# Token tiles 2 to 9 loaded in a transposed layout as well, with 1/rms spread by one small product

## The chip, the core and the metric

The kernel runs on one core of one Trainium2 chip. The core has a matrix engine (TensorE, PE in the profile, with its weight loads as PEld), a vector engine (DVE), a scalar engine (ACT), GpSimd (POOL) and a queue that issues DMAs (SP). The metric is device time in microseconds, the median of several executions. All data are float32. Many products are split into three: a value is held as a high part that PE multiplies fast (fp32r) and a low part, the rest, and high x high, high x low and low x high are added up.

## The reference, cut to what matters

One layer of a backbone block: 1024 latent tokens (x) and 256 context tokens (ctx), 1024 channels. What the change touches is its first step, the norm and modulation ahead of the input projection:

```
def rms_norm(x, g):
    y = xf * lax.rsqrt(jnp.mean(xf * xf, axis=-1, keepdims=True) + EPS)
    return (y * g).astype(x.dtype)

def modulate(h, shift, scale):
    return h * (1.0 + scale) + shift

px = modulate(rms_norm(x, g_pre_mix), sh_m, sc_m) @ w_in
pc = modulate(rms_norm(ctx, g_pre_mix), csh_m, csc_m) @ w_in
...   (window attention and mLSTM on px and pc, output projection, SwiGLU)
```

scale and shift come from a conditioning vector through w_ada and are vectors over channels; 1/rms is one number for each token.

## The kernel before, in words

The opening stage reads w_ada, makes `scol` = g (1 + scale) and `hcol` = shift as columns over channels, and prepares the tokens in ten tiles of 128 (0 to 7 are x, 8 and 9 are ctx). The projections need the tokens transposed, channels on the partitions. For each tile i:

- `prep_a`: a DMA loads `xt` (128 tokens x 1024 channels). ACT squares it with a running sum (Square; the squares themselves go to `hraw` as waste) and takes the root, DVE the reciprocal: column 10+i of `st` is 1/rms of each token. POOL multiplies `xt` by it (for tile 2 ACT does it in `prep_a2`, for tile 3 POOL at L434).
- `prep_t`: PE transposes the eight 128x128 blocks of `xt` into two PSUM tiles `pt`.
- `prep_m`: DVE multiplies them by `scol` into `hraw` (L231, two halves of 128x512).
- `prep_b`: POOL adds `hcol` (L244, two halves; tiles 0 and 1 on DVE), ACT casts each half to the high part `hh` (`ch` for ctx), DVE subtracts for the low part `hl` (`cl`, L257). hh0, hl0 hold the first four channel blocks, hh1, hl1 the other four.

After that PE multiplies the tile with the first 272 columns of the projection (`s1`: 24 products into a PSUM tile `slab`, L77 to L79 in `mm3`, with `w1h`, `w1l`); DVE adds the gates' bias (`G`, L396 and L398), ACT copies the rest (`av`, `V`, L400 and L401). The next 384 columns (`s2`, `w2h`, `w2l`) fill in between, first half and second half of the channels apart. Their weights come by DMA in four pieces `wr384` and are split by ACT (L448) and DVE (L449).

Python issues tile i's product, prep_b of tile i+2 and prep_a of tile i+4 in one loop step (L423 on), but the order on each engine is set by a scheduler at build time, which works with its own estimates of durations; only instructions marked `keep_in_program_order` hold their place among each other. On the chip each engine runs its list in that order and waits at the head of it. SBUF buffers R4 to R15 are shared by tag: `xt` has R4 to R7, `hraw` R8 to R13 from tile 2 on, which held w_ada before, and the pieces of w2 R14 and R15. DMAs are issued by SP in order; one whose buffer is still read holds up those behind it. `tc.issue_after` puts a DMA behind another.

Of the kernel before, what the change touches and what calls it, by code (L numbers as in the profile page):

```python
# [9 lines left out]
F32 = mybir.dt.float32  # L10
F32R = mybir.dt.float32r
AF = mybir.ActivationFunctionType
ALU = mybir.AluOpType
PSUM = bass.MemoryType.PSUM
ADD, SUB, MUL, MAX, MIN = ALU.add, ALU.subtract, ALU.mult, ALU.max, ALU.min

P = 128
D = 1024
KT = D // P
S = 1024  # L20
NT = S // P
# [20 lines left out]
WSPLIT = {1: 3, 2: 6, 3: 7, 5: 0, 6: 4, 7: 1, 8: 2, 9: 5}  # L42


def body(tc, x, ctx, vecs, bcv, bada, gqm, gqf, wada, ws1, ws2, wt, wout, wfi, wfo,
         const, cosc, sinc, out):
    nc = tc.nc
    pe, act, dve, pool = nc.tensor, nc.scalar, nc.vector, nc.gpsimd
# [36 lines left out]
    def hcast(t, n=4, w=P):  # L85

        return t.rearrange("p (h o) -> p h o", o=1).broadcast_to([t.shape[0], n, w])
# [94 lines left out]
        act.activation(dst, ss, AF.Sqrt, bias=epst, scale=1.0 / D)  # L182
        dve.reciprocal(dst, dst)

    def prep_a2(i):
        tc.keep_in_program_order(act.activation(xts[i], xts[i], AF.Copy, scale=st[:, 10 + i:11 + i]))

    def prep_a(i, parts=(0, 1)):

        j = i - NT  # L190
        xt = xts[i] = R(4 + i % 4, f"xt{i}", (D,))
        xd[i] = dma(xt, x[i * P:(i + 1) * P] if i < NT else ctx[j * P:(j + 1) * P])
        hraw[i] = R((2, 3)[i] if i < 2 else (12, 13, 8, 9, 10, 11)[i % 6], f"hraw{i}", (KT, P))
        sq = act.activation(hraw[i].rearrange("p a b -> p (a b)"), xt, AF.Square, accum_out=st[:, i:i + 1])
        if i > 1:
            tc.keep_in_program_order(sq)
        if 1 not in parts:
            tc.keep_in_program_order(act.activation(st[:, 10 + i:11 + i], st[:, i:i + 1], AF.Sqrt, bias=epst, scale=1.0 / D))
            return
        rms_r(st[:, 10 + i:11 + i], st[:, i:i + 1])  # L200
        pool.tensor_scalar(xt, xt, st[:, 10 + i:11 + i], 1.0, MUL, MUL)

    pts = {}

    def prep_t(i, keep=False, parts=(0, 1)):

        xt = xts[i]
        for b in parts:
            pt = pa.tile([P, 4, P], F32, name="pt", tag="tp" if i else "mm", bufs=2 if i else 4)
            for k in range(4):  # L210
                kk = 4 * b + k
                t = pe.transpose(pt[:, k, :], xt[:, kk * P:(kk + 1) * P], ident)
                if keep and (not kk or i == 1):
                    tc.keep_in_program_order(t)
            pts.setdefault(i, []).append(pt)
# [3 lines left out]
    def prep_m(i):  # L219

        if i not in pts:
            prep_t(i)
        rw = hraw.pop(i)
        raw2[i] = [rw[:, 4 * b:4 * b + 4] for b in range(2)]
        for b in range(2):
            if i == 1 and not b:
                for k in range(4):
                    tc.keep_in_program_order(act.activation(raw2[i][b][:, k], pts[i][b][:, k], AF.Copy,
                                                                    scale=scol[:, 0, 4 * b + k:4 * b + k + 1]))
                continue  # L230
            r = dve.tensor_tensor(raw2[i][b], pts[i][b], hcast(scol[:, i // NT, 4 * b:4 * b + 4]), MUL)  # L231
            if i == 1:
                tc.keep_in_program_order(r)

    def prep_b(i):

        if i not in raw2:
            prep_m(i)
        q, j = (0, i) if i < NT else (1, i - NT)
        hs, ls = (hh, hl) if i < NT else (ch, cl)  # L240
        tok = slice(j * P, (j + 1) * P)
        raws_ = raw2.pop(i)
        for b in (1, 0) if i == 0 else range(2):
            r = (dve if i < 2 else pool).tensor_tensor(raws_[b], raws_[b], hcast(hcol[:, q, 4 * b:4 * b + 4]), ADD)  # L244
            if i < 2:
                tc.keep_in_program_order(r)
            if i == 0:
                w1_split(1, (1 - b,))
        for b in range(2):
            h_ = hs[b][:, :, tok]  # L250
            if i + b == 0:
                for k in range(4):
                    act.activation(h_[:, k], pts[i][b][:, k], AF.Identity, scale=scol[:, q, k:k + 1],
                                   bias=hcol[:, q, k:k + 1])
            else:
                tc.keep_in_program_order(act.copy(h_, raws_[b]))
            r = dve.tensor_tensor(ls[b][:, :, tok], raws_[b], h_.bitcast(F32), SUB)  # L257
            if i == 0:
                tc.keep_in_program_order(r)
        if i == 0:  # L260
            with tc.issue_after(last):
                prep_a(2, (0,))
            r2 = st[:, 12:13]
            tc.keep_in_program_order(dve.reciprocal(r2, r2))
            prep_a2(2)

    def slab_load(hi, lo, src, n, k0):
        for k in (0, 2):
# [154 lines left out]
    for i in range(NI):  # L423
        if i + 4 < NI:
            prep_a(i + 4)
        if i == 0:
            s1(i)
            prep_t(2, True)
        if i + 2 < NI:
            prep_b(i + 2)  # L430
        if i == 0:
            r = st[:, 13:14]
            dve.reciprocal(r, r)
            tc.keep_in_program_order(pool.tensor_scalar(xts[3], xts[3], r, 1.0, MUL, MUL))  # L434
        if i:
            s1(i)
        if i == 4:
            for m_, c_ in ((mF, up), (mB, lw)):
                tc.keep_in_program_order(dve.tensor_scalar(m_, c_, -1.0, -NEG, ADD, MUL))
        if i in (1, 2):  # L440
            b = i - 1
            w2h.append(w2_tile("h", b, f"w2h_{b}").rearrange("p (k n) -> p k n", k=4))
            w2l.append(w2_tile("l", b, f"w2l_{b}").rearrange("p (k n) -> p k n", k=4))
            with tc.issue_after(xd[i + 4].ins):
                for k in (0, 2):
                    raw = R(14 + k // 2, f"wr384_{k}", (2, 384))
                    dma(raw, ws2[:, b, k:k + 2])
                    tc.keep_in_program_order(act.copy(w2h[b][:, k:k + 2], raw))  # L448
                    dve.tensor_tensor(w2l[b][:, k:k + 2], raw, w2h[b][:, k:k + 2].bitcast(F32), SUB)  # L449
        if 3 <= i < 3 + 2 * NFILL:  # L450
            s2((i - 3) // 2, ((i - 3) % 2,))
# [1484 lines left out]
def pack(i):  # L1936
    a = {k: np.asarray(v) for k, v in i.items()}
    w = a["w_in"][0]
    aqw, akw, avw, mqw, mkw, mvw, mow, mgw = np.split(w, np.cumsum([512, 128, 128, 256, 256, 512, 512]), axis=1)
    cc = np.ascontiguousarray  # L1940

    def slab(z):
        return cc(z.reshape(2, 4, P, -1).transpose(2, 0, 1, 3))

    tiles = {}
    for j in range(4):
        tiles[f"aq{j}"] = np.concatenate([aqw[:, 64 * j:64 * j + 64], aqw[:, 256 + 64 * j:256 + 64 * j + 64]], 1)
        tiles[f"mo{j}"] = mow[:, 128 * j:128 * j + 128]
    for j in range(2):
        tiles[f"mq{j}"] = mqw[:, 128 * j:128 * j + 128]  # L1950
        tiles[f"mk{j}"] = mkw[:, 128 * j:128 * j + 128]
    tiles["ak"] = akw

    def ttile(z):
        return z.reshape(KT, P, P).transpose(1, 0, 2)

    conv = a["w_conv_qk"][0]
    vec = np.concatenate(
        [np.stack([a["c"][0].reshape(KT, P), a["c_ctx"].reshape(KT, P)], 0).transpose(2, 1, 0).reshape(P, 16),
         conv.reshape(3, 4, P).transpose(2, 1, 0).reshape(P, 12),  # L1960
         a["g_mlstm_out"][0].reshape(4, P).T]
        + [a["b_ada"][0].reshape(6, KT, P)[i].T for i in (0, 1, 3, 4)]
        + [a[k][0].reshape(KT, P).T for k in ("g_pre_mix", "g_pre_ffn")] + [np.eye(P, dtype=np.float32)], 1)
    wo = a["w_out"][0]
    wop = np.stack([np.concatenate([wo[64 * j:64 * j + 64], wo[256 + 64 * j:256 + 64 * j + 64]], 0) for j in range(4)]
                   + [wo[512 + 128 * j:640 + 128 * j] for j in range(4)], 0)
    fi = a["w_ffn_in"][0].reshape(KT, P, 2, HT, P).transpose(3, 2, 1, 0, 4)
    con, cos, sin = _consts()
    return {
        "x": cc(a["x"][0]), "ctx": cc(a["ctx"][0]), "vecs": cc(vec),  # L1970
        "bcv": np.concatenate([a["b_gates"][0], a["attn_sink"][0]])[None, :],
        "bada": cc(a["b_ada"]), "gqm": cc(a["g_post_mix"]), "gqf": cc(a["g_post_ffn"]),
        "wada": cc(a["w_ada"][0]),
        "ws1": slab(np.concatenate([mgw, avw, mvw[:, :128]], 1)), "ws2": slab(mvw[:, 128:]),
        "wt": cc(np.stack([ttile(tiles[n]) for n in TILES], 0)),
        "wout": cc(wop), "wfi": cc(fi), "wfo": cc(a["w_ffn_out"][0].reshape(HT, P, D)),
        "const": con, "cosc": cos, "sinc": sin,
    }
# [11 lines left out]
```

## Time and profile before

| | |
|---|---|
| three runs | 1181.67, 1182.40, 1182.69 us; median 1182.4 |
| profiled execution | 1181.93 us, span 1180.2 us, mean granted PE clock 0.998 |
| PE, PEld busy | 1161.6 us (98%), 948.0 us (80%) |
| DVE, ACT, POOL busy | 781.8 us (66%), 558.0 us (47%), 154.0 us (13%) |
| DMA | 214.89 MB, mean 182 GB/s |

The span is the time from the first to the last instruction of one execution under the profiler; all rows are from that execution. The token tiles are prepared between about 20 and 80 us of it. A row of the timeline gives start and length in us, engine, line, operation, output<-inputs, shapes, count, and in brackets how long the engine had been idle before it and what ended that. Lines are those of the kernel before.

### The profile page before, as it was taken

The numbers are of one execution on the slowest core, as the hardware profiler recorded it, in microseconds if no ns is written. First come the engines' busy times: TensorE is split into PE (matmuls) and PEld (weight loads), VectorE is DVE, ScalarE is ACT, GpSimd is POOL, SyncE is SP. The second block draws the span as 40 slices with busy tenths as digits, with TensorE's granted clock in tenths as the row PEclk, the third lists the DMA queues.
The fourth block names the chain that finished last, engine by engine and source line by source line (L and its number), as shares of the span: only waits on it lengthen the run. The fifth ranks groups of instructions, "written<-read, shape, count | busy, mean of one in ns | idle before, by whom it ended". The sixth has DMA issues, their size and how long they took to land.

```text
span 1180.2 us, 16216 instructions
## 1 busy us (share of the span) xinstructions
PE 1161.6 (98%) x5881; PEld 948.0 (80%) x5881; DVE 781.8 (66%) x1367; ACT 558.0 (47%) x1035; POOL 154.0 (13%) x204
## 2 busy tenths in 40 slices
PE   9899999999999999999999999999999999999997
PEld 3799888778787777888788888888888888888886
DVE  5863768872877752559767767777777755644566
ACT  6743442221776864887433333333333434434543
POOL 1550001225555550000000000000000000000000
PEclk9999999999999999999999999999999999999999
DMA  9611954747885733220344565655654558665853
GB/s 367 218 54 51 382 201 138 217 122 224 220 257 158 220 98 118 88 92 36 98 134 130 202 239 207 221 197 205 219 173 135 178 191 272 207 212 184 310 184 125
DMA packets 101992, 214.89 MB, mean 182 GB/s; under 512 B 10004, under 2 KB 39316, under 8 KB 100504
## 3 DMA queue, kind: packets, MB, share of 16 engines
q1 hardware_dynamic: 101912, 213.85, 54.9%
q8 instruction: 46, 0.75, 0.3%
q14 instruction: 34, 0.28, 0.1%
HBM read 157.19 MB, written 55.97 MB: 181 GB/s over the span
## 4 chain that ended last, share of the span: by engine, by line
PE 89%; DMA 4%; DVE 4%; ACT 1%; issue 1%; SPq 0%; POOL 0%; DVEq 0%; ACTq 0%
PE xv L79 8%; PE xv L77 8%; PE xv L78 8%; PE pt L77 6%; PE pt L78 6%; PE pt L79 6%; PE po L1019 3%; PE t L597 3%; PE t L596 3%; PE t L599 3%; PE pt L1001 3%; PE op L77 3%; PE op L79 2%; PE op L78 2%; PE fx L77 2%; PE slab L77 2%
## 5 line engine op out<-in xcount | busy, mean ns | idle before, releaser
L66 DVE TENSOR_TENSOR fo<-fr,fo 128x1024 fp32r<-128x1024 f32 x77 | 92.7, 1223 | 70.4 <-ACT fo L65 65.9
L65 ACT CAST fo<-fr 128x1024 fp32r<-128x1024 f32 x77 | 79.8, 1053 | 73.8 <-PE pt L79 33.1
L596 PE MATMUL t<-hh,th 128*128 128x512 f32 x208 | 82.4, 396 | 0.0
L597 PE MATMUL t<-hl,th 128*128 128x512 f32 x208 | 82.1, 395 | 0.0
L1396 ACT CAST wS<-wr 128x512 fp32r<-128x512 f32 x88 | 54.3, 624 | 55.2 <-PE pt L79 36.6
L1398 DVE TENSOR_TENSOR wS<-wr,wS 128x512 fp32r<-128x512 f32 x88 | 60.4, 689 | 19.8 <-ACT wS L1396 19.8
L77 PE MATMUL xv<-tT,wS 128*128 128x512 f32 x168 | 65.6, 391 | 0.0
L79 PE MATMUL xv<-tT,wS 128*128 128x512 f32 x168 | 65.6, 391 | 0.0
L78 PE MATMUL xv<-tT,wS 128*128 128x512 f32 x168 | 65.5, 390 | 0.0
L599 PE MATMUL t<-hh,tl 128*128 128x512 f32 x208 | 65.0, 393 | 0.0
L77 PE MATMUL op<-woh,mh 128*128 128x512 f32 x128 | 51.1, 399 | 0.0
L79 PE MATMUL op<-woh,ml 128*128 128x512 f32 x128 | 50.0, 391 | 0.0
L78 PE MATMUL op<-wol,mh 128*128 128x512 f32 x128 | 49.9, 390 | 0.0
L1144 DVE TENSOR_TENSOR wr<-wr 128x512 f32<-128x512 f32 x66 | 45.5, 689 | 1.4
L596 PEld LDWEIGHTS t<-hh,th 128*128 128x128 f32 x208 | 39.1, 188 | 8.3 <-issue 0.3
L597 PEld LDWEIGHTS t<-hl,th 128*128 128x128 f32 x208 | 39.1, 188 | 8.1 <-issue 1.4
L1430 ACT ACTIVATE es<-es 128x512 f32<-128x512 f32 x22 | 13.9, 634 | 66.5 <-DVE es L1147 66.5
L78 PE MATMUL pt<-fo 128*128 128x512 f32 x110 | 42.8, 389 | 0.0
L77 PE MATMUL pt<-fo 128*128 128x512 f32 x110 | 42.8, 389 | 0.0
L79 PE MATMUL pt<-fo 128*128 128x512 f32 x110 | 42.8, 389 | 0.0
L972 PE MATMUL s<-k,qh 128*128 128x256 f32 (+1 forms) x128 | 42.2, 339 | 0.6 <-DVE sm L974 0.5
L599 PEld LDWEIGHTS t<-hh,tl 128*128 128x128 f32 x208 | 37.3, 188 | 6.6 <-issue 0.3
(786 smaller groups left out, 3341.0 us busy)
## 6 DMA issues: line engine op xcount, KB each, us to landing
wr<-in_wfi SPq DMA_DIRECT2D x44, 512.0 KB, 4.5
wb<-in_wada SPq DMA_DIRECT2D x24, 512.0 KB, 5.6
s_d<-a SPq DMA_DIRECT2D x22, 512.0 KB, 6.8
bt<-in_wfo SPq DMA_DIRECT2D x44, 256.0 KB, 3.6
tb_d<-bt SPq DMA_DIRECT2D x11, 1024.0 KB, 3.9
fr<-s_d SPq DMA_DIRECT2D x44, 256.0 KB, 4.5
fr<-tb_d SPq DMA_DIRECT2D x44, 256.0 KB, 4.3
fr<-a_d SPq DMA_DIRECT2D x33, 256.0 KB, 3.7
```

Source lines behind the costliest of these rows:

```text
L65: act.copy(hi, raw)
L66: dve.tensor_tensor(lo, raw, hi.bitcast(F32), SUB)
L77: pe.matmul(ps, a[0], b[0], start=first, stop=False, **kw)
L78: pe.matmul(ps, a[0], b[1], start=False, stop=False, **kw)
L79: pe.matmul(ps, a[1], b[0], start=False, stop=last, **kw)
L596: pe.matmul(o, wh[:, kt], m[0], start=f, stop=False)
L597: pe.matmul(o, wh[:, kt], m[1], start=False, stop=False)
L599: pe.matmul(o, wl[:, kt], m[0], start=False, stop=l)
L972: pe.matmul(o, qh[:, h, :], k2[g][:, kc], start=True, stop=False)
L1144: dve.tensor_tensor(out, a, b, SUB)
L1396: act.copy(w[:, 0], raw)
L1398: dve.tensor_tensor(w[:, 1], raw, w[:, 0].bitcast(F32), SUB)
```

## The change

For tiles 2 to 9 a second copy of the tokens comes from memory in transposed layout (`xtr`, made when the inputs are packed: per tile 128 partitions x 8 channel blocks x 128 tokens, 512 KB) straight into `hraw`. `xt` is loaded as before, but only for the sum of squares, and Square writes its waste over `xt`. The eight transposes are replaced by one product: the column of 1/rms, spread over 128 columns, times the identity gives a PSUM tile in which every partition holds the 128 tokens' 1/rms. DVE multiplies all of `hraw` by it in one instruction (128x1024), and POOL does scale and shift at once, in eight instructions of 128x128, one for each channel block, with `scol` and `hcol` as its two column operands. The multiplications of `xt` by 1/rms go. Tiles 0 and 1 stay as they are.

```diff
-def body(tc, x, ctx, vecs, bcv, bada, gqm, gqf, wada, ws1, ws2, wt, wout, wfi, wfo,
+def body(tc, x, ctx, xtr, vecs, bcv, bada, gqm, gqf, wada, ws1, ws2, wt, wout, wfi, wfo,
...
-    def prep_a2(i):
-        tc.keep_in_program_order(act.activation(xts[i], xts[i], AF.Copy, scale=st[:, 10 + i:11 + i]))
     def prep_a(i, parts=(0, 1)):
...
-        sq = act.activation(hraw[i].rearrange("p a b -> p (a b)"), xt, AF.Square, accum_out=st[:, i:i + 1])
+        if i > 1:
+            xd[i] = dma(hraw[i], xtr[i])
+        sq = act.activation(xt if i > 1 else hraw[i].rearrange("p a b -> p (a b)"), xt, AF.Square, accum_out=st[:, i:i + 1])
...
-        pool.tensor_scalar(xt, xt, st[:, 10 + i:11 + i], 1.0, MUL, MUL)
+        if i < 2:
+            pool.tensor_scalar(xt, xt, st[:, 10 + i:11 + i], 1.0, MUL, MUL)
     def prep_t(i, keep=False, parts=(0, 1)):
         xt = xts[i]
+        if i > 1:
+            pts[i] = pa.tile([P, 4, P], F32, name="pt", tag="tp", bufs=2)[:, 0]
+            t = pe.matmul(pts[i], st[:, 10 + i:11 + i].broadcast_to([P, P]), ident, start=True, stop=True)
+            if keep:
+                tc.keep_in_program_order(t)
+            return
...
         raw2[i] = [rw[:, 4 * b:4 * b + 4] for b in range(2)]
+        if i > 1:
+            dve.tensor_tensor(rw, rw, pts[i].rearrange("p (o t) -> p o t", o=1).broadcast_to([P, KT, P]), MUL)
+            return
...
-            r = (dve if i < 2 else pool).tensor_tensor(raws_[b], raws_[b], hcast(hcol[:, q, 4 * b:4 * b + 4]), ADD)
-            if i < 2:
-                tc.keep_in_program_order(r)
+            if i > 1:
+                for k in range(4):
+                    kk = 4 * b + k
+                    pool.tensor_scalar(raws_[b][:, k], raws_[b][:, k], scol[:, q, kk:kk + 1], hcol[:, q, kk:kk + 1], MUL, ADD)
+                continue
+            tc.keep_in_program_order(dve.tensor_tensor(raws_[b], raws_[b], hcast(hcol[:, q, 4 * b:4 * b + 4]), ADD))
...
-            prep_a2(2)
...
-            tc.keep_in_program_order(pool.tensor_scalar(xts[3], xts[3], r, 1.0, MUL, MUL))
...
+        "xtr": cc(np.concatenate([a["x"][0], a["ctx"][0]], 0).reshape(NT + NC_, P, KT, P).transpose(0, 3, 2, 1)),
```

The scheduler's order changes on all engines in this stage; behind it every engine's list is the same as before. Names carry the number of the tile or piece, and slab_442, slab_564 and slab_628 are the first products of tiles 1, 3 and 4 after the change.

DVE around the low parts of tile 2, before (slab_448 is tile 1, the two pt are tile 3's transposes):

```order
L396 TENSOR_TENSOR G_92<-slab_448,bcr_60 128x2x4
L257 TENSOR_TENSOR hl0_103<-hraw2_350,hh0_101 128x4x128
L398 TENSOR_TENSOR G_92<-slab_448,bcr_60 128x2x4
L183 RECIPROCAL st_67<-st_67 128x1
L257 TENSOR_TENSOR hl1_104<-hraw2_350,hh1_102 128x4x128
L449 TENSOR_TENSOR w2l_0_478<-wr384_0_479,w2h_0_477 128x768
L231 TENSOR_TENSOR hraw3_363<-pt_430,scol_68 128x512
L231 TENSOR_TENSOR hraw3_363<-pt_435,scol_68 128x512
L449 TENSOR_TENSOR w2l_0_478<-wr384_2_483,w2h_0_477 128x768
```

And after:

```order
L409 TENSOR_TENSOR G_92<-slab_442,bcr_60 128x2x4
L232 TENSOR_TENSOR hraw3_363<-hraw3_363,pt_427 128x1024
L269 TENSOR_TENSOR hl0_103<-hraw2_350,hh0_101 128x4x128
L183 RECIPROCAL st_67<-st_67 128x1
L269 TENSOR_TENSOR hl1_104<-hraw2_350,hh1_102 128x4x128
L183 RECIPROCAL st_67<-st_67 128x1
L232 TENSOR_TENSOR hraw4_370<-hraw4_370,pt_488 128x1024
L269 TENSOR_TENSOR hl0_103<-hraw3_363,hh0_101 128x4x128
L407 TENSOR_TENSOR G_92<-slab_503,bcr_60 128x2x4
L409 TENSOR_TENSOR G_92<-slab_503,bcr_60 128x2x4
L232 TENSOR_TENSOR hraw5_422<-hraw5_422,pt_549 128x1024
L459 TENSOR_TENSOR w2l_0_472<-wr384_0_473,w2h_0_471 128x768
```

The multiplication of the next tile now stands ahead of the low part that PE needs, and the first w2 piece comes three tiles' multiplications later.

DVE around the second half of w2 (w2l_1), before:

```order
L257 TENSOR_TENSOR hl1_104<-hraw3_363,hh1_102 128x4x128
L449 TENSOR_TENSOR w2l_1_542<-wr384_0_543,w2h_1_541 128x768
L231 TENSOR_TENSOR hraw5_425<-pt_558,scol_68 128x512
L231 TENSOR_TENSOR hraw5_425<-pt_563,scol_68 128x512
L449 TENSOR_TENSOR w2l_1_542<-wr384_2_547,w2h_1_541 128x768
L257 TENSOR_TENSOR hl0_103<-hraw4_369,hh0_101 128x4x128
```

And after, where slab_628 is tile 4's product:

```order
L407 TENSOR_TENSOR G_92<-slab_628,bcr_60 128x2x4
L409 TENSOR_TENSOR G_92<-slab_628,bcr_60 128x2x4
L449 TENSOR_SCALAR mF_64<-cst_58 128x128
L449 TENSOR_SCALAR mB_65<-cst_58 128x128
L459 TENSOR_TENSOR w2l_1_533<-wr384_0_534,w2h_1_532 128x768
L269 TENSOR_TENSOR hl0_103<-hraw6_483,hh0_101 128x4x128
L269 TENSOR_TENSOR hl1_104<-hraw6_483,hh1_102 128x4x128
L459 TENSOR_TENSOR w2l_1_533<-wr384_2_538,w2h_1_532 128x768
```

The splits of w2_1 moved from ahead of tile 4's low parts to behind G of tile 4's product.

PE at the same place, after:

```order
L79 MATMUL slab_628<-w1h1_118,hl1_104 128x272
L77 MATMUL slab_593<-w2h_1_532,hh1_102 128x384
L78 MATMUL slab_593<-w2l_1_533,hh1_102 128x384
L79 MATMUL slab_593<-w2h_1_532,hl1_104 128x384
L77 MATMUL slab_593<-w2h_1_532,hh1_102 128x384
```

PE takes up w2_1 with the instruction that follows tile 4's last product; ACT has the copy of tile 4's product (`av`) ahead of the cast of w2h_1 in the same way. On SP the eight new loads stand among the old ones, four of them ahead of tile 4's `xt`, six ahead of the first piece of w2.

## The prediction

> **What bounds the kernel now.** I read the page's busy table and chain first, then the windows of the opening 90 us, then who waited for whom there, and last the engines' timelines. In the fence stand the busy table, the shares of the chain that ended last, four windows (their columns: stretch, length, busy us and count of PE, PEld, DVE, ACT and POOL, PE clock, DMA share, GB/s) and the six waits of PE and of its weight loads (PEld) between 39 and 62 us (total, times, longest).
>
> ```profile
> PE 1161.6 (98%) x5881; PEld 948.0 (80%) x5881; DVE 781.8 (66%) x1367; ACT 558.0 (47%) x1035; POOL 154.0 (13%) x204
> ...
> PE 89%; DMA 4%; DVE 4%; ACT 1%; issue 1%; SPq 0%; POOL 0%; DVEq 0%; ACTq 0%
> ...
> 30.00:40.00 10.00, 8.27 (x46) 6.40 (x43) 8.21 (x20) 8.68 (x17) 0.11 (x1) 0.83 0.72 280
> 40.00:50.00 10.00, 8.30 (x67) 7.82 (x65) 7.82 (x14) 8.69 (x21) 6.66 (x6) 1.00 0.29 87
> 50.00:60.00 10.00, 9.62 (x66) 9.06 (x66) 9.33 (x14) 5.92 (x12) 9.57 (x7) 1.00 0.74 256
> 60.00:70.00 10.00, 9.95 (x76) 9.67 (x75) 9.93 (x21) 7.16 (x17) 8.80 (x7) 1.00 0.01 2
> ...
> PEld slab L79 <- DVE hl L257: 2.0, 2, 1.7
> PE slab L79 <- DVE hl L257: 1.5, 1, 1.5
> PEld slab L78 <- DVE w2l L449: 0.7, 1, 0.7
> PEld slab L77 <- ACT hh L256: 0.5, 1, 0.5
> PE slab L78 <- DVE w2l L449: 0.4, 1, 0.4
> PE slab L77 <- ACT hh L256: 0.2, 1, 0.2
> ```
>
> TensorE is the bound of the whole: 98% busy, 89% of the chain. What leaves its queue in the opening stage leaves the end, as long as nothing else makes it wait. From 40 to 60 us it does wait, 2.1 us by the PE rows (1.5 + 0.4 + 0.2) and 3.2 us by the weight loads (2.0 + 0.7 + 0.5). I take 2.7 us as what the old waits cost. The waits are for DVE, and DVE and POOL are both nearly full from 50 to 70 us (9.33 and 9.93, 9.57 and 8.80 of 10). So this stage balances on three engines, and PE's relief counts only where DVE's order follows it.
>
> **PE's work.** PE's timeline of the opening stage: start, length, instruction, count.
>
> ```profile
> 1.06 4.59 PE L297 MATMUL warm<-ones 128*128 128x128 f32 x22 [1.06 <-POOL ones L110]
> ...
> 69.92 0.37 PE L77 MATMUL slab<-w1h,hh 128*128 128x272 f32 x1
> 70.13 0.28 PE L78 MATMUL slab<-w1l,hh 128*128 128x272 f32 x1
> 70.25 0.30 PE L79 MATMUL slab<-w1h,hl 128*128 128x272 f32 x1
> ...
> 75.13 1.04 PE L212 MATMUL pt<-vec,xt 128*128 128x128 f32 x8
> 75.92 0.37 PE L77 MATMUL slab<-w1h,hh 128*128 128x272 f32 x1
> ...
> 79.01 0.34 PE L77 MATMUL slab<-w2h,hh 128*128 128x384 f32 x1
> ...
> 81.10 0.28 PE L77 MATMUL slab<-w1h,ch 128*128 128x272 f32 x1
> ```
>
> Eight transposes hold PE 0.79 us (75.13 to 75.92). The first matmul behind them takes 0.21 us to the next start (69.92 to 70.13) where the following one takes 0.12, so 0.88 us per tile. A tile's 24 products with w1 then take 3.09 us (75.92 to 79.01), 0.126 each behind the first, and half a tile's 12 products with w2 take 2.09 us (79.01 to 81.10), 0.174 each. The new product is one fp32 128x128 matmul, which is recorded as two passes (the 11 warm-up products are 22 records). Lower bound: two passes at the transposes' 0.10 us, 0.20. Upper: two at the warm-up's 4.59 / 22 = 0.21, 0.42. The shape of operand and output is that of the transposes and the clock there was full, so I stay near the lower end: 0.25, with restart 0.30. Saved: 8 x (0.88 - 0.30) = 4.6 us; ends 8 x (0.79 - 0.42) = 3.0 and 8 x (0.88 - 0.20) = 5.4.
>
> **The chain of a tile.** DVE and ACT instructions, POOL groups (busy, mean ns) and one DMA row (KB each, median us to landing).
>
> ```profile
> L257 DVE TENSOR_TENSOR hl<-hraw,hh x14: 668/926/1536, 39.5 to 71.0; 128x512 fp32r<-128x512 f32 x14
> ...
> L449 DVE TENSOR_TENSOR w2l<-wr,w2h x4: 959/1596/1843, 46.6 to 56.8; 128x768 fp32r<-128x768 f32 x4
> ...
> 40.10 0.69 DVE L231 TENSOR_TENSOR hraw<-pt,scol 128x512 f32<-128x512 f32 x1
> ...
> 60.04 0.15 DVE L396 TENSOR_TENSOR G<-slab,bcr 128x8 f32<-128x8 f32 x1
> ...
> 81.77 1.23 DVE L66 TENSOR_TENSOR tl<-tw,th 128x1024 fp32r<-128x1024 f32 x1 [1.12 <-ACT th L65]
> ...
> 42.32 0.62 ACT L256 CAST hh<-hraw 128x512 fp32r<-128x512 f32 x1
> ...
> 52.32 0.84 ACT L448 CAST w2h<-wr 128x768 fp32r<-128x768 f32 x1 [0.67 <-DMA wr<-in_ws]
> ...
> 60.35 0.27 ACT L400 COPY av<-slab 128x128 f32<-128x128 f32 x1
> ...
> L244 POOL TENSOR_TENSOR hraw<-hraw,hcol 128x512 f32<-128x512 f32 x16 | 20.5, 1302 | 11.0 <-DVE hraw L231 11.0
> ...
> L201 POOL TENSOR_SCALAR xt<-xt,st 128x1024 f32<-128x1024 f32 x8 | 11.8, 1475 | 22.7 <-DVE scol L354 19.8 <-DVE st L183 2.1 <-POOL xt L434 0.8
> L988 POOL TENSOR_SCALAR pr__4387<-pr__4387,sm 128x640 f32<-128x640 f32 x4 | 3.6, 913 | 0.2 <-DVE sm L985 0.2
> ...
> L795 POOL TENSOR_SCALAR bcr<-bcr 128x8 f32<-128x8 f32 x1 | 0.2, 204 | 0.0
> ...
> wr<-in_ws SPq DMA_DIRECT2D x4, 384.0 KB, 7.7
> ```
>
> POOL: a tile cost 1.48 for x times 1/rms and 2 x 1.30 for the shift, 4.1 us. Now it is eight scalar instructions of 128 columns. No row has that with two column operands; between 0.20 us at 8 columns and 0.91 at 640 it comes to 0.34, so 2.7 us a tile. Ends: 0.20, which is 1.6 us, and 0.91, which is 7.3. It is nearest to the short row; I take 2.7. POOL becomes the lighter engine, and its chain of a tile stays as long as before (2.7 against 2.6). Cover for it: DVE reaches the tile's low part only after the next tile's product, as below. Gone, the cover would cost what the third rival says.
>
> DVE: two halves of 0.69 from PSUM become one instruction over 1024 columns, about 1.23 by the row of that size, so the work is equal. But the scheduler has put it elsewhere, and that makes new waits on PE. hl is the low half of a tile, the third operand of each group of three products.
> 1. Tile 1: the whole product of tile 2 stands ahead of tile 1's second low part, 1.23 where one half (0.69) stood: 0.3 us (0 to 0.5).
> 2. Tile 2: G of tile 1, which waits for PE's last product of it, then the product of tile 3, then tile 2's low part: 0.15 + 1.23 + 0.67 to 0.93 = 2.1 us, less two products that PE still has: 1.9 us (1.5 to 2.1).
> 3. Tile 3: the same with the product of tile 4, but PE has half a tile in hand: 0.3 us (0 to 0.6).
> 4. First w2 half: G, the product of tile 5, then w2l (0.96 to 1.60): 2.3 to 3.0 us, while PE has 13 products (1.6): 1.0 us (0.7 to 1.4).
> 5. Second w2 half: on ACT its cast stands behind the copy of tile 4's product, on DVE its low part behind G of tile 4; both wait for PE to finish tile 4, and PE's next instruction needs both. Copy 0.27, cast 0.84, low part 0.96 to 1.60: 2.4 us (2.1 to 2.7). Before, these splits stood ahead of tile 4.
> 6. Its second piece: two low parts of tile 6 and w2l, 2 x 0.67 + 0.96 = 2.3 us at the least, against six products (1.0): 1.1 us (0.9 to 2.0).
>
> New waits 7.0 us (5.2 to 9.3), old ones 2.7 (2.1 to 3.2), all of which they replace. After that I see none: tiles 5 and 6 are ready long before PE comes to them. Stage sum: 7.0 - 2.7 - 4.6 = -0.3 us; ends -3.4 and +4.2.
>
> **The clock.** Windows, columns as above.
>
> ```profile
> 32.00:34.00 2.00, 0.71 (x9) 0.53 (x8) 1.43 (x6) 1.45 (x4) 0.11 (x1) 1.00 1.04 405
> ...
> 35.50:37.00 1.50, 1.50 (x8) 1.48 (x8) 1.50 (x4) 1.31 (x3) 0.00 (x0) 0.58 0.89 345
> 37.00:38.00 1.00, 1.00 (x6) 1.00 (x5) 1.00 (x4) 0.53 (x1) 0.00 (x0) 0.50 0.11 40
> ...
> 43.00:46.00 3.00, 1.54 (x13) 1.32 (x12) 2.35 (x5) 2.43 (x7) 2.16 (x3) 1.00 0.05 20
> ```
>
> After 32 to 34 us, where PE was busy 0.71 of 2, the granted clock fell to 0.58 and 0.50, to about 39 us. After 43 to 46, busy 1.54 of 3, it did not. Waits 5 and 6 leave PE idle for some 3.5 of 5.6 us, nearer to the first. One such fall of 3.5 us at half speed would cost up to 1.7 us, none 0. I take half, 0.9 us.
> The Trainium skill (TensorE: Matmul & The Clock Gate, section "Why this matters for your kernels") says to avoid PE gaps above about 3 us between bursts, since one idle window brings the half clock. By that rule no wait here is long enough and the time would be 1182.1 us. The trace disagrees: PE was idle 1.73 us in the whole of 30 to 40 us (8.27 busy of 10), and the clock fell there, so I do not go by it.
>
> **The loads.** Eight more loads of 512 KB are 4.2 MB. At the 30 to 40 us row's 280 GB/s at 0.72 share (390 at full) that is 10.8 us of transport, and rows 40:50 and 60:70 have room for it (0.29 and 0.01 busy). On the queue four of them stand ahead of tile 4's x, 2.1 MB or 5.4 us, and six ahead of the first w2 load, 8 us. The cover is that the queue was quiet from 37 us on (40 GB/s) and w2 was first split at 46.6 us (the w2l row). I cost it at nothing; the fourth rival has it uncovered. ACT's scaling of tile 2 goes too; the wait for DVE in 1 takes its place and is costed there.
>
> **Sum.** -0.3 + 0.9 = +0.6 us on the profiled 1181.93 us (span 1180.2 and 1.7 around it), 1182.5. That run stands 0.5 under the median of 1182.4, inside the three runs' 1181.67 to 1182.69; on the median the forecast is 1183.0 us. A measurement here can tell 0.2%, 2.4 us, from no change, so this is no change.
>
> **Rivals.**
> - Faster: the loads come early enough and the low parts in time, the new waits shrink to the old 2.7 us, and PE's 4.6 us go through: 1177.8, or 1179 with part of it. For it: PE is the bound, POOL gets lighter, and less POOL work means DVE runs nearer to 0.67 than 1.54 per low part. Against: waits 5 and 2 are fixed by the order, not by speed. Chance 0.20.
> - Slower by the clock: two or three half-speed stretches, each up to 1.7 us, at waits 2, 4 and 5: 1182.4 - 0.3 + 3.4 = 1185.5. Decides from about half idle in a stretch of 3.5 us. Chance 0.14.
> - Slower by POOL: with 0.55 us a piece POOL takes 4.4 a tile and tile 6's low part, behind four tiles in its queue, comes 4 x 1.7 = 6.8 us later, less one tile's 2.7 in hand: 1182.4 + 4.1 = 1186.5. The 0.91 us row speaks for it, the 0.20 against. Chance 0.05.
> - Slower by DMA: the second w2 pieces start only when the first are split, and at 7.7 us to landing they would prolong wait 5 or 6 by 3 us: 1182.4 - 0.3 + 3.0 = 1185.1. Chance 0.05.
>
> No change keeps 0.56. Faster 0.20, slower 0.14 + 0.05 + 0.05 = 0.24. The range 1179.0 to 1186.0 leaves out half of the first rival and the worst ends of the slower ones. The forecast's own is 1180.0 to 1184.8.
>
> **What would show it.** PE's L212 group gone but for tiles 0 and 1, and a product per tile of about 0.25 us. PE's waits in the first 90 us up from 2.1 to some 6 us, the longest on w2l and w2h behind tile 4's product. POOL rows of about 0.34 us. A window near 62 us with a clock below 1. G of tile 9 on DVE at about 89 us, as before. I am wrong if PE is above 9.5 of 10 from 50 us on (then it is faster), or if PE waits on ACT's cast of hh behind POOL (then slower).

## The result, and the profile after

The change made the kernel slower: 1184.78 us (median of 11 runs, 1183.62 to 1186.1) against 1180.85 us for the kernel before (11 runs, 1179.73 to 1182.69). The ratio is 1.0032, 95% interval 1.0024 to 1.0040, so it lies just above the 0.2% that a measurement here can tell from no change. The profiled execution of after took 1185.27 us with a span of 1183.3 us, 3.1 us longer than the span before.

The busy table and the shares of the chain that ended last, of the page of after; then four windows with the columns known from before; then PE's waits from 39 to 95 us (engine, tile and line <- releaser: total us, times, longest):

```profile
PE 1161.4 (98%) x5833; PEld 946.7 (80%) x5833; DVE 775.2 (66%) x1359; ACT 556.0 (47%) x1034; POOL 159.1 (13%) x245
...
PE 91%; DMA 3%; ACT 2%; POOL 2%; DVE 1%; issue 1%; SPq 0%; DVEq 0%; ACTq 0%; POOLq 0%
...
40.00:50.00 10.00, 7.92 (x57) 7.07 (x57) 7.13 (x15) 6.88 (x19) 9.44 (x18) 1.00 1.03 399
50.00:60.00 10.00, 7.96 (x55) 7.32 (x53) 6.19 (x15) 6.35 (x15) 10.00 (x18) 1.00 0.51 176
60.00:70.00 10.00, 7.03 (x21) 5.86 (x22) 6.43 (x9) 7.08 (x15) 3.82 (x7) 0.56 0.17 52
70.00:80.00 10.00, 10.00 (x68) 10.00 (x68) 4.65 (x10) 2.91 (x7) 9.38 (x19) 0.93 0.37 106
...
PE slab L77 <- ACT w2h L458: 3.8, 2, 1.9
PE slab L79 <- DVE hl L269: 1.7, 3, 0.9
PE slab L78 <- DVE w2l L459: 1.2, 3, 0.7
PE slab L77 <- ACT hh L268: 0.5, 1, 0.5
```

PE has 48 matmul records fewer and yet the same busy time: from 60 to 70 us it ran 21 matmuls where before it ran 76, at a granted clock of 0.56. DVE, which was full from 50 to 70 us before, is down to 6.2 and 6.4 of 10; POOL is full from 40.6 to 63.6 us. PE waits 7.2 us (3.8 + 1.7 + 1.2 + 0.5) where it waited 2.1, and the longest waits are on the second half of w2. Two engines show how these come about. PE's timeline from the end of tile 4's product, ACT's in the same stretch (each row: start, length, instruction, and in brackets how long the engine had been idle and who ended that):

```profile
57.86 0.29 PE L79 MATMUL slab<-w1h,hl 128*128 128x272 f32 x1
60.09 0.45 PE L77 MATMUL slab<-w2h,hh 128*128 128x384 f32 x1 [1.94 <-ACT w2h L458]
61.23 0.69 PE L78 MATMUL slab<-w2l,hh 128*128 128x384 f32 x1 [0.70 <-DVE w2l L459]
...
65.08 0.69 PE L77 MATMUL slab<-w2h,hh 128*128 128x384 f32 x1 [1.88 <-ACT w2h L458]
66.07 0.69 PE L78 MATMUL slab<-w2l,hh 128*128 128x384 f32 x1 [0.31 <-DVE w2l L459]
```

```profile
59.04 0.27 ACT L411 COPY av<-slab 128x128 f32<-128x128 f32 x1 [0.42 <-DVE G L409]
59.20 0.83 ACT L458 CAST w2h<-wr 128x768 fp32r<-128x768 f32 x1
61.53 0.62 ACT L268 CAST hh<-hraw 128x512 fp32r<-128x512 f32 x1 [1.50 <-POOL hraw L256]
...
63.68 0.62 ACT L268 CAST hh<-hraw 128x512 fp32r<-128x512 f32 x1 [1.36 <-POOL hraw L256]
64.20 0.83 ACT L458 CAST w2h<-wr 128x768 fp32r<-128x768 f32 x1
...
66.31 0.60 ACT L268 CAST hh<-hraw 128x512 fp32r<-128x512 f32 x1
```

The first cast of w2's second half (59.20) stands in ACT's list behind the copy of tile 4's product (59.04), which can't start before PE has finished that product; and PE's next instruction needs the cast. The second cast (64.20) stands behind both casts of tile 6 (61.53 and 63.68, each released by POOL), although PE needs tile 6 only after tile 5, whose own casts come last of all (66.31). So PE waits for w2, ACT waits for POOL, and the tile that POOL is working on is not wanted yet.

POOL's group of the new instruction from 30 to 100 us (busy us, mean ns | idle), its stretch for tiles 2 to 6, the new product with the matmul ahead of it and behind it on PE, and G of tile 9 on DVE, after and, in the last line, before:

```profile
L256 POOL TENSOR_SCALAR hraw<-hraw,scol,hcol 128x128 f32<-128x128 f32 x64 | 36.1, 578 | 16.3 <-DVE hraw L232 16.3
...
40.56 23.08 POOL L256 TENSOR_SCALAR hraw<-hraw,scol,hcol 128x128 f32<-128x128 f32 x40 [7.55 <-DVE hraw L232]
...
46.17 0.38 PE L210 MATMUL pt<-vec,st 128*128 128x128 f32 x2
46.30 0.37 PE L77 MATMUL slab<-w1h,hh 128*128 128x272 f32 x1
46.51 0.28 PE L78 MATMUL slab<-w1l,hh 128*128 128x272 f32 x1
...
93.79 0.17 DVE L407 TENSOR_TENSOR G<-slab,bcr 128x8 f32<-128x8 f32 x1 [3.93 <-PE slab L79]
...
89.40 0.17 DVE L396 TENSOR_TENSOR G<-slab,bcr 128x8 f32<-128x8 f32 x1 [4.85 <-PE slab L79]
```

A piece on POOL took 0.58 us, eight pieces 4.6 us a tile (23.08 / 5), against 4.1 us before. G of tile 9 came at 93.79 us, 4.4 us later than before (89.40). PE's rows keep that lag up to 235 us of the span; by 500 us it is 3.2. What PE runs there is the same in both kernels, and ten of the eleven other profiles gain on the one of before in that stretch, so most likely that one execution was slow there (its 1181.93 us lie 1.1 above the median). The 4.4 us, not the 3.1 between the spans, are what the stage lost.

### The profile page after: what moved, and what is told of

Read it like the earlier page. It is cut to its first block, busy times and chain, and to the rows that moved or that the text cites. A ratio compares the mean times of both kernels' runs of the same rounds, so it can differ in the third digit from the quotient of the medians.

```text
span 1183.3 us, 16172 instructions
## 1 busy us (share of the span) xinstructions
PE 1161.4 (98%) x5833; PEld 946.7 (80%) x5833; DVE 775.2 (66%) x1359; ACT 556.0 (47%) x1034; POOL 159.1 (13%) x245
## 4 chain that ended last, share of the span: by engine, by line
PE 91%; DMA 3%; ACT 2%; POOL 2%; DVE 1%; issue 1%; SPq 0%; DVEq 0%; ACTq 0%; POOLq 0%
PE xv L79 8%; PE xv L78 8%; PE xv L77 8%; PE pt L79 6%; PE pt L77 6%; PE pt L78 6%; PE t L607 4%; PE t L606 4%; PE t L609 4%; PE op L77 2%; PE op L79 2%; PE op L78 2%; PE po L1029 2%; PE pt L1011 2%; PE fx L77 2%; PE fx L79 2%
## 5 line engine op out<-in xcount | busy, mean ns | idle before, releaser
L66 DVE TENSOR_TENSOR fo<-fr,fo 128x1024 fp32r<-128x1024 f32 x77 | 92.8, 1222 | 71.1 <-ACT fo L65 68.1
```

The source lines that it names most:

```text
L66: dve.tensor_tensor(lo, raw, hi.bitcast(F32), SUB)
```

## The experiments

The theory after this reading: the work saved on PE is real, and it is eaten by an order of instructions. The scheduler put w2's second half behind tile 4's product and tile 6 ahead of tile 5; the waits that follow are long enough to halve PE's clock, and POOL's eight instructions make the second of them longer. Rivals: the extra loads cost by their transport; POOL's price alone carries the loss; the waits on w2 are bound by late pieces of w2 in shared buffers and not by the order.

**The loads alone.**

```diff
...
         hraw[i] = R((2, 3)[i] if i < 2 else (12, 13, 8, 9, 10, 11)[i % 6], f"hraw{i}", (KT, P))
+        if i > 1:
+            xd[i] = dma(hraw[i], xtr[i])
         sq = act.activation(hraw[i].rearrange("p a b -> p (a b)"), xt, AF.Square, accum_out=st[:, i:i + 1])
```

> The kernel before, with the eight extra loads of 512 KB put into hraw and overwritten there by Square; transposes, scaling and shift stay as before. The loads alone move the scheduler's order: both splits of the second half of w2 stand behind tile 4's product, and tile 6's casts ahead of tile 5's, as after the change. Theory (the order made by the loads costs, not their transport): about 7 us of PE waits in place of 2.7 and a half-speed stretch of 3 us, with nothing saved on PE: 1180.9 + 7.5 = 1188 us (1185 to 1191), and no wait for a DMA of more than 0.5 us. Rival, POOL's eight short instructions carry the loss: no change, 1180.9. Rival, transport: the same time as by the order, but with PE or ACT waiting for DMA.

1186.49 us, ratio 1.0051 (1.0039 to 1.0064): 5.9 us over its 1180.55 of before, with none of the new arithmetic in it. PE's waits from 39 to 95 us:

```profile
PE slab L77 <- ACT w2h L450: 2.1, 2, 1.5
PE slab L78 <- DVE w2l L451: 1.7, 2, 1.2
PE slab L79 <- DVE hl L259: 0.4, 1, 0.4
PE slab L77 <- ACT hh L258: 0.3, 1, 0.3
```

The waits on w2's second half are there: 0.55 us on its first low part, then 1.51 and 1.17 us at its second piece (the other 0.55 on w2h is for the first half). Its second cast came at 62.72 us, behind the copy of tile 4's product (62.41), as the theory said; its first, at 59.09, did not stand behind that copy, though the expectation had it there. In all PE waited 4.5 us where about 7 were expected, with one half-speed stretch of 3.4 us. Neither PE nor ACT waited for a DMA from 39 to 75 us. POOL's old instructions were in place, so POOL's new price isn't needed for a loss.

**The waits filled.** Idle products in PE's three gaps.

```diff
+            warm(11)                      # ahead of s2(0, second half); each 128x384, 0.17 us
...
+                    warm(3)               # behind its first product
...
+                    warm(13)              # ahead of its second piece
```

> The kernel after, with 27 idle products (0.17 us each, to a PSUM tile that nothing reads) pinned into PE's three waits on the second half of w2: 11 ahead of it, 3 behind its first product, 13 ahead of its second piece; 4.7 us of work in some 5.5 us of waits. Theory: the half clock from 60.9 to 71.1 us costs about 3 us of the result by itself; PE stays busy, the clock stays at 1.00, and the time falls from 1184.8 to about 1181.8 us (1181 to 1183). Rival, the waits alone cost and the half clock lies beside them: 1184.8, or up to 0.5 more.

1182.81 us, ratio 1.0020 (1.0011 to 1.0029), with 4.7 us of additional work on PE. The window and G of tile 9:

```profile
60.00:70.00 10.00, 8.75 (x48) 7.78 (x48) 6.67 (x9) 7.04 (x15) 4.17 (x8) 1.00 0.18 52
...
91.40 0.17 DVE L407 TENSOR_TENSOR G<-slab,bcr 128x8 f32<-128x8 f32 x1 [1.78 <-PE slab L79]
```

The clock stays at 1.00, and tile 9 comes 2.4 us earlier than after (93.79). So the half clock cost 2.0 us by the medians (1.7 when each is taken against its own runs of before) and 2.4 by this row; the 3 us expected were too many. The intervals of the two ratios touch (after begins at 1.0024), so the size is known to about a microsecond, while the row and the clock leave no doubt of the effect.

**Own buffers for the second half of w2.**

```diff
-                    raw = R(14 + k // 2, f"wr384_{k}", (2, 384))
+                    raw = R(14 + k // 2 if b == 0 else (0, 3)[k // 2], f"wr384_{k}", (2, 384))
```

> The kernel after, with the two pieces of the second half of w2 loaded into buffers R0 and R3, free by then, in place of R14 and R15, where they wait until the first half is split. With that the scheduler puts these splits ahead of tile 4's product and tile 5's casts ahead of tile 6's. Theory (the order costs): the two waits on w2's second half (4.8 us) and the half-speed stretch behind them (3 us) go, less new waits of 1 to 3 us on tiles 4 and 5: 1184.8 - 6 = 1179 us (1177 to 1180.5), faster than before. Rival, POOL's 4.6 us a tile is the bound of this stage: PE waits on ACT's casts and DVE's low parts behind POOL instead, 1183 to 1185.

1176.50 us, ratio 0.9968 (0.9956 to 0.9981): 4.1 us faster than before and 8.3 faster than after, 0.5 us below the range that the theory gave. Windows and PE's waits from 39 to 95 us:

```profile
50.00:60.00 10.00, 9.81 (x69) 9.50 (x67) 7.67 (x12) 7.74 (x18) 10.00 (x14) 1.00 0.59 227
60.00:70.00 10.00, 9.71 (x71) 9.52 (x70) 6.36 (x15) 6.29 (x14) 10.00 (x18) 1.00 0.05 6
...
PE slab L79 <- DVE hl L269: 1.4, 2, 0.9
PE slab L77 <- ACT hh L268: 0.5, 1, 0.5
PE pt L210 <- DVE st L183: 0.3, 1, 0.3
PE slab L78 <- DVE w2l L459: 0.2, 1, 0.2
```

POOL is as full as after (10.00 and 10.00 of 10), and PE is at 9.8 and 9.7: POOL's price alone is not the bound once its tiles are asked for in the order in which it makes them; 2.4 us of PE's waits are left.

**Tiles 6 to 9 alone.**

```diff
-        if i > 1:
+        if i >= 6:       # in the load, the product, DVE's and POOL's instructions; tiles 2 to 5 as before
```

> The change on tiles 6 to 9 alone; tiles 2 to 5 go as before. The order up to tile 5's product is that of before. Theory: four tiles save 0.66 us of PE each, 2.6 us, no new wait on w2 and no new half-speed stretch: 1180.9 - 2.6 = 1178.3 us (1177.5 to 1179.5). Rival, POOL's eight short instructions: its queue of 4.6 us a tile makes tile 6 late, and the time is that of before, 1180.9, or more.

1178.52 us, ratio 0.9979 (0.9970 to 0.9988): 2.0 us gained with four tiles, inside the range given. PE waited 1.4 us on a low part, 1.0 on w2, where no new wait was expected, and 0.2 on hh: 0.5 more than before, about the 0.6 by which the gain fell short of the 2.6 forecast, though the interval is 1 us to either side.

**Order alone, first part.** Edges that only order instructions on ACT and DVE (`behind`), with after's loads and buffers.

```diff
+        if i == 4:
+            behind(c_, w2c[-1])        # copy of tile 4's product behind w2's second cast
+            behind(g_, w2s[-1])        # G behind its low part
...
+                if i in (5, 6):
+                    behind(c_, w2c[-1])    # casts of tiles 5 and 6, and their low parts likewise
```

> The kernel after with its buffers and loads as they are; only order edges are added: on ACT the copy of tile 4's product and the casts of tiles 5 and 6, on DVE G of tile 4 and the low parts of tiles 5 and 6 stand behind both splits of w2's second half. Theory (the order costs, the load had landed in time): its pieces are issued at 51.2 and 52.8 us and split by about 57 us, the waits of 1.9 + 0.7 + 1.9 + 0.3 us and the half-speed stretch go: 1179 us (1177.5 to 1181). Rival, the load is late in these buffers and only the earlier one in e3 helped: ACT's cast waits for the DMA and PE behind it, 1183 to 1185.

1183.23 us, ratio 1.0019 (1.0010 to 1.0028): by the time, the rival's. By the trace it is neither; PE's rows:

```profile
60.00 0.45 PE L77 MATMUL slab<-w2h,hh 128*128 128x384 f32 x1 [1.25 <-ACT w2h L469]
60.99 0.44 PE L78 MATMUL slab<-w2l,hh 128*128 128x384 f32 x1 [0.55 <-DVE w2l L470]
...
66.50 0.40 PE L77 MATMUL slab<-w1h,hh 128*128 128x272 f32 x1 [1.95 <-ACT hh L268]
```

The second wait on w2 is gone, but a wait of 1.95 us on hh has taken its place: tile 5's casts still stood behind tile 6's, and these behind POOL. The first was shorter by 0.7 us only because PE came to it later: the cast itself, still behind tile 8's Square, started at 59.13 us against 59.20 in after. ACT waited for no piece of w2. The edges had left half of the order as it was.

**Order alone, whole.**

```diff
+        if i == 8:
+            behind(sq, w2c[-1])            # tile 8's Square behind w2's casts
...
+                    if i == 6:
+                        behind(c_, last5[2])   # tile 6's casts behind tile 5's; low parts likewise
```

> e5 with the rest of the order of e3 as well: the Square of tile 8 also stands behind the splits of w2's second half, and tile 5's casts and low parts ahead of tile 6's. Buffers and loads are those of after. Theory (order alone): the splits run at 56 to 58 us if the pieces have landed, tile 5's casts no longer stand behind tile 6's four POOL pieces, and of the waits from 58 to 66 us some 1 us is left: 1180 us (1178.5 to 1181.5). Rival, the pieces land too late in these buffers: ACT waits for DMA there, 1182 to 1184.

1178.13 us, ratio 0.9977 (0.9969 to 0.9986), 0.4 us below the range expected. ACT's casts of w2's second half, and PE's waits from 39 to 95 us:

```profile
57.63 0.85 ACT L477 CAST w2h<-wr 128x768 fp32r<-128x768 f32 x1
59.01 0.83 ACT L477 CAST w2h<-wr 128x768 fp32r<-128x768 f32 x1 [0.53 <-DMA wr<-in_ws]
...
PE slab L79 <- DVE hl L276: 1.6, 3, 0.9
PE slab L78 <- DVE w2l L478: 0.8, 2, 0.6
PE slab L77 <- ACT hh L270: 0.5, 1, 0.5
PE pt L212 <- DVE st L183: 0.4, 1, 0.4
```

Same loads, same buffers, same arithmetic as after, and 6.7 us less (1184.8 to 1178.1): the order was the loss. A wait for DMA does appear, of 0.5 us at the second piece. From here to e3 it is another 1.6 us; the load comes earlier there and the order differs too, and no run tells these apart.

**The edit of e3 without the change, and with the loads only.**

> The kernel before with the edit of e3 alone (R0 and R3 for the second half of w2). Its splits stood ahead of tile 4's product already. Theory: at most the 0.4 us wait on w2's low part goes: 1180.3 us (1179.5 to 1181), the same. Rival, the buffers are worth by themselves what e3 gained: 1176.5 to 1177.5.

> The kernel of e1 (before, with the eight extra loads) with the edit of e3. The splits stand ahead of tile 4's product again. Theory (loads cost by the order they cause, not by transport): the 5.9 us of e1 shrink to 0 to 2: 1181 us (1180 to 1183). Rival, transport: still 1185 to 1187, with waits for DMA.

e6: 1180.51 us, ratio 1.0001 (0.9992 to 1.0010), the same as before, so the buffers bring nothing by themselves. e7: 1179.74 us, 0.9992 (0.9983 to 1.0001), 6.8 us less than e1 by one line, and 0.3 below the range expected. 4.2 MB more on the queue cost nothing where the order is kept. Two windows of e7 (the last two columns are DMA share and GB/s), and all its waits of PE from 39 to 95 us:

```profile
40.00:50.00 10.00, 9.12 (x72) 8.48 (x71) 7.32 (x18) 7.83 (x22) 8.93 (x8) 1.00 1.03 403
...
60.00:70.00 10.00, 10.00 (x80) 9.97 (x80) 9.65 (x18) 7.20 (x17) 7.94 (x8) 1.00 0.01 2
...
PE slab L77 <- ACT w2h L450: 0.5, 1, 0.5
PE slab L78 <- DVE w2l L451: 0.4, 1, 0.4
PE slab L79 <- DVE hl L259: 0.3, 1, 0.3
```

e7 less e3 is 3.2 us, the worth of the new arithmetic with the loads and the buffers given.

**Tile 2's scale and shift on DVE,** in e3 and in after.

```diff
-                    pool.tensor_scalar(raws_[b][:, k], ...
+                    (dve if i == 2 else pool).tensor_scalar(raws_[b][:, k], ...
```

> The kernel of e3, with tile 2's eight scale-and-shift instructions on DVE (about 0.25 us each by the 128x128 rows of mF and mB) in place of POOL (0.58). POOL's queue starts with tile 3 and every later tile is 2 to 4.6 us earlier. Theory (what is left of POOL's price is PE's 1.4 us for tile 2 and 0.5 for tile 3): 1176.5 - 1.3 = 1175.2 us (1174.3 to 1176.3). Rival, DVE is the bound of that stretch: its 2 us more put the products of tiles 3 and 4 later, 1176.5 to 1178.

> The kernel after, with tile 2's scale and shift on DVE; buffers as in after. POOL's queue is one tile (4.6 us) shorter up to tile 6, while both splits of w2's second half still stand behind tile 4's product. Theory (POOL's price reached the end through ACT's list: tile 6's cast waits for POOL and w2's second piece stands behind it): PE's second wait of 1.9 us goes and the half-speed stretch is shorter by one or two of its three windows, the first wait of about 2 us stays: 1182 us (1180.5 to 1183.5). Rival, POOL has no share: the same as after, 1184.3 to 1185.3.

e8: 1176.52 us, 0.9964 (0.9952 to 0.9977), the same as e3: PE's waits on hl went from 1.4 to 0.7 us, and one of 0.7 us for G on DVE came, as the rival said. e10: 1183.51 us, 1.0020 (1.0011 to 1.0030), 1.3 us less than after, with the window and PE's first row of waits:

```profile
60.00:70.00 10.00, 7.74 (x28) 6.39 (x28) 5.70 (x9) 6.91 (x13) 5.20 (x10) 0.66 0.18 56
...
PE slab L77 <- ACT w2h L458: 2.9, 3, 1.4
```

So POOL's price had a small share at most: the first wait on w2's second half fell from 1.94 to 1.23 us, the second from 1.88 to 1.41 and not to zero, the half-speed stretch from 10.2 to 6.8 us. The interval touches that of after, and the scheduler moved another instruction as well: w2's first cast (58.83 us) now stands ahead of the copy of tile 4's product (59.55), which the expectation did not have. How much of the 1.3 us is POOL's and how much that order's stays open. The version to keep is e3, one line on top of the change.

## Why the prediction was right or wrong

The forecast was no change with 0.56, at 1183.0 us; slower had 0.24. It came out slower, inside the range. As a difference the forecast was +0.6 us and the result +3.9 (medians of 11) or +3.1 (spans); later runs put the kernel before 1.5 us under the three on which the forecast stood.

- **PE's work saved**, 4.6 us (3.0 to 5.4). The new product takes 0.13 us to the next start and 0.21 for that one, where a matmul otherwise follows in 0.126: 0.34 - 0.126 = 0.21 us a tile, so 8 x (0.88 - 0.21) = 5.4 us, the upper end.
- **The new waits**, 7.0 us. PE's rows give 7.2, term by term: tile 1 0.2 (0.3 forecast), tile 2 0.52 + 0.92 = 1.4 (1.9), tile 3 0.5 (0.3), first half of w2 0.2 (1.0), second half behind tile 4's product 1.94 + 0.70 = 2.6 (2.4), its second piece 1.88 + 0.31 = 2.2 (1.1). The order said where they would be, and the fifth, the largest, was right. But the 2.7 us of old waits were the middle between PE's rows and the weight loads', and on that footing the new ones are 8.8 (7.2 and 10.3), 1.8 us more than forecast. By PE's rows alone PE waited 7.2 - 2.1 = 5.1 us more than before, against the 7.0 - 2.7 = 4.3 forecast.
- **The second piece** was the term that failed in its reasoning. It counted DVE's low parts of tile 6, and not that ACT's cast of w2 stands behind tile 6's casts, which wait for POOL. "If PE waits on ACT's cast of hh behind POOL (then slower)" named the sign of it; it came one instruction on, at the cast of w2 behind that of hh.
- **POOL**, 0.34 us a piece, 2.7 a tile. It was 0.58 and 4.6, near the 0.55 of the third rival; 0.44 of that is the piece by itself, as the last section shows. That it lies beside DVE's work was wrong in after and nearly right in e3, where PE waits 2.4 us. The rival's mechanism did come, but e10, which takes 4.6 us out of POOL's queue, gains 1.3 us at the most, not 4.1: the late tile was not wanted at once.
- **The clock**, 0.9 us for one stretch. There were three, without a break, from 61.1 to 71.4 us. e2 puts them at 2.0 to 2.4 us, less than the 1.7 us each of the second rival, because part of the slow products lay ahead of a wait that ACT's second cast ended anyway: the second piece started at 65.08 us in after and at 65.14 in e2. The trace was the better guide than the rule by which no wait was long enough: the longest was 1.94 us, and the clock fell. Of the same page of the Trainium skill (TensorE: Matmul & The Clock Gate) the section "A second HAM failure mode: psum-queue depth-cycling" fits better; it says that PE pausing briefly but often between groups of matmuls is enough to make the clock go back and forth. This trace agrees with the fall: waits of 1.94 and 0.70 us between groups, and then a clock of 0.50; it shows one fall and one return, no going back and forth.
- **The loads**, 0 us. Right for their transport (e7), wrong for the change as a whole: by e1 it is the loads that move the order. The prediction costed the new order and didn't ask which of the parts had caused it.

The measured terms can be added up from PE's rows of after: 5.1 us more of waits, 5.4 us of work saved, and for the half clock about 4.0 us, half of the 1.97 + 2.56 + 3.41 us that PE was busy at 0.50 (not e2's 2.0 to 2.4, as the waits of after are those left behind the slow products). That is 5.1 - 5.4 + 4.0 = +3.7 us, against 4.4 at G of tile 9; about 0.7 us is in none of the terms.

## What to carry to other kernels

Where a scheduler sets the order, a new load is also a change of order for everything whose data come behind it on the queue; compare each engine's list with and without the loads alone before pricing the arithmetic. Read a wait not only by its releaser but by what stands ahead of the releaser in its own list: here PE waited for a cast of w2, that cast for a tile which nobody needed yet, and one line that gave w2 its own buffers turned a loss of 0.3% into a gain of 0.3%. When PE has to wait, many short waits can cost the clock as well, so their price is more than their sum.

## What the runs showed of the hardware

The half clock came in steps of 3.4 us: 3.4 in e1 and e5, 6.8 in e10, 10.2 in after. Windows of after, cut at these steps:

```profile
57.71:61.12 3.41, 0.88 (x5) 0.40 (x3) 1.82 (x7) 1.87 (x5) 3.41 (x8) 1.00 0.01 2
61.12:64.53 3.41, 1.97 (x5) 1.46 (x5) 0.97 (x3) 1.64 (x4) 2.52 (x5) 0.50 0.50 154
64.53:67.95 3.42, 2.56 (x7) 2.17 (x8) 2.62 (x5) 3.39 (x7) 0.00 (x0) 0.50 0.00 0
67.95:71.36 3.41, 3.41 (x14) 3.41 (x13) 3.15 (x4) 2.15 (x5) 1.54 (x2) 0.50 0.00 0
```

The step after a window with PE busy 0.88 us of 3.4 ran at half, and so did those after 1.97 and 2.56 us at half clock; after a full one the clock came back. The other falls followed 0.72 (e1), 1.60 (e5) and 1.60 us (e10), and the returns 3.15 (e1), 3.14 (e5) and 3.40 us (e10); a stretch of 3.4 us with PE busy 1.94 us in before (42.0 to 45.4) brought no fall. So PE half idle in one such step was enough to lose the clock for the next, with no single wait of more than 1.94 us, and it took a step nearly full of work to get it back.

A piece of 128x128 on POOL with two column operands had a median of 446 ns and a mean of 578. The trace of after shows where the rest comes from: 49 of the 64 pieces took 0.44 to 0.48 us, and the 15 that took 0.82 to 1.66 all overlapped a subtraction on DVE that reads two tensors from SBUF (a low part, L66, L269 or L459) for 0.5 us or more, and ended 0.16 to 0.32 us behind one. Nine pieces that lay wholly beside L232, which reads one of its operands from PSUM, took 0.44 to 0.45. So some 0.13 us of the mean 0.58 is time in which POOL stood behind DVE.
